# First modulation in one-tile groups, with repacked weights and zero products on TensorE

## The chip, the cores and the metric

The kernel runs on one core of one Trainium2 chip. The core has TensorE (PE, matrix products), VectorE (DVE), ScalarE (ACT), GpSimd (POOL) and SyncE (SP, which here only issues DMAs). The metric is the device time of one execution in microseconds (us). "Before" is given as the median of three runs.

## What is computed

The reference is a two-layer backbone over 256 latent tokens and 256 context tokens, with 1024 features. Layer 0 mixes tokens with a bidirectional mLSTM, layer 1 with latent attention; each is followed by a gated ConvFFN. Every sub-layer's input is first modulated by a shift and a scale that come from a condition vector. The change concerns the first of these modulations and the first matrix product behind it:

```python
ml = silu(c)     @ ada_w[0] + ada_b[0]    # 6 rows of 1024: shift, scale, gate, ...
mc = silu(c_ctx) @ ada_w[0] + ada_b[0]
hl = x   * (1 + ml[1]) + ml[0]
hc = ctx * (1 + mc[1]) + mc[0]
x_m = h @ w_up                             # h: hc and hl, 512 tokens; w_up: 1024 x 2048
```

## The kernel before

All activations are kept transposed: features on the 128 partitions, the 512 tokens along the free axis, so the 1024 features are eight *feature tiles*. Each fp32 product is made of three fp32r products (`mm3`, lines 312 to 314): both operands are split into a high part, which ACT makes by a cast (line 317), and a low part, which DVE makes by a subtraction (line 318); then high x high, high x low, low x high are accumulated.

The opening stage is `start_up`. It makes the modulation's shift and scale for all eight feature tiles, modulates the tokens, and meanwhile computes the first five (`NUP`) of the sixteen output tiles of `w_up`, called up 0 to up 4 here. The tiles of features are taken in four groups of two (`GROUPS`). For a group g the steps are:

- `S`: split the group's modulation weights. They are 1 MB a feature tile (1024 inputs x 128 features x shift and scale), so two SBUF tiles of 128x1024 a feature tile, four a group; each takes one ACT cast and one DVE subtraction (`ada_split`).
- `A`: products of the condition (as a stationary operand of 4 columns) with these parts, and a copy of the 4-row result out of PSUM by ACT (`ada_rows`, lines 402 and 405). The products have 512 columns for a group of two tiles; there are 16 of them.
- `T`: tiny transposes on TensorE that turn the rows into columns (`ada_T`, line 412).
- `M`: two small DVE additions (lines 422, 423), then for each feature tile the modulation itself (DVE for the context half, line 500; ACT for the latent half, line 502) and its split into `hT` (`mod_tiles`, `h_split`).
- `W` m: split of the weights of up m.
- two digits gm: the products of up m with the feature tiles of group g, three a feature tile.

In `start_up`, the strings `LOADS` and `STEPS` are orders written out by hand. `LOADS` is the order in which SP issues the loads: `a` g the modulation weights of group g, `x` g the transposed tokens of its tiles (256 KB each), `r` m the weights of up m (512 KB). `STEPS` is the order of work, and inside `manual_schedule` the queues of PE, DVE and ACT each hold their instructions in just this order; an instruction that waits holds up all that stand behind it on its engine. The modulation weights are read from `ada_w` as eight transfers of 256 KB a group, in pieces of 1 KB. `setup` loads the small parameters (`sm`) through SP's queue.

When the products of the five up tiles are done, `w_up` goes on with the other eleven, and from there on TensorE works nearly without a gap.

Of the kernel before, what the change touches and what calls it, by code (L numbers as in the profile page):

```python
# [7 lines left out]
F32 = mybir.dt.float32  # L8
F32R = mybir.dt.float32r
# [5 lines left out]
D = 1024  # L15
# [10 lines left out]
H1 = 8  # L26
# [5 lines left out]
NB, NRAW, NU = 3, 3, 31  # L32
# [9 lines left out]

NUP = 5
GROUPS = ((0, 2), (2, 4), (4, 6), (6, 8))
LOADS = [(c[0], int(c[1])) for c in "a0 r0 r1 x0 r2 a1 r3 r4 x1 a2 x2 x3 a3".split()]
STEPS = [(c[0], int(c[1])) for c in (
    "S0 W0 A0 T0 M0 W1 W2 S1 00 01 W3 W4 A1 03 T1 M1 02 04 10 11 S2 A2 12 T2 M2 13 14 21 "
    "S3 20 A3 24 T3 22 23 M3 31 32 33 34 30").split()]  # L50

TAIL = {"mout": 4, "fout0": 6, "aout": 7, "fout1": 6}
WIDE = {"mout": 5, "fout0": 6, "aout": 7, "fout1": 10}
# [67 lines left out]
def _pack(i):  # L121
    ids, _ = _plan()
    ws = np.zeros((len(ids), 128, CW), np.float32)
# [14 lines left out]
    for key, (n, cols) in ids.items():  # L138
        kind, a, c = key
        if kind == "up":  # L140
            b = _stat(i["m_w_up"][0], a, 0, 8)
        elif kind == "og":
            b = _mov(i["m_w_og"][0][:, a * 512:(a + 1) * 512], 2 * c, 2)
        elif kind == "gates":
            b = _stat(gz, 0, 8 * c, 8)
        elif kind == "v":
            b = _mov(i["m_w_v"][0][:, a * 512:(a + 1) * 512], 2 * c, 2)
        elif kind == "qk":
            b = _stat(i["m_w_qk"][0], a, 8 * c, 8)
        elif kind == "mout":  # L150
            b = _mov(i["m_w_out"][0], c, 1)
        elif kind in ("fin0", "fin1"):
            b = _stat(i["ffn_w_in"][int(kind[-1])], a + NF * c, 0, 8)
        elif kind in ("fout0", "fout1"):
            b = _mov(i["ffn_w_out"][int(kind[-1])], c, 1)
        elif kind == "dkv":
            b = _mov(i["a_w_dkv"][0], dkv_s[c], cols // 320)
        elif kind == "dq":
            b = _mov(i["a_w_dq"][0], 2 * c, 2)
        elif kind == "ukn":  # L160
            b = kn_blocks[:, c * 1024:(c + 1) * 1024]
        elif kind == "uv":
            b = _mov(uv, c, 1)
        elif kind == "uqn":
            b = qn_blocks[:, c * 1024:(c + 1) * 1024]
        elif kind == "uqr":
            b = _mov(uqr, 2 * c, cols // 512)
        elif kind == "aout":
            b = _mov(i["a_w_out"][0], c, 1)
        ws[n, :, :cols] = b  # L170

    def col(a):
        a = np.asarray(a)
        k = a.shape[-1] // 128
        a = a.reshape(a.shape[:-1] + (k, 128))
        return np.moveaxis(a, -1, 0).reshape(128, -1)
# [16 lines left out]
    for k, v in parts.items():  # L193
        off[k] = (o, v.shape[1])
        o += v.shape[1]
    sm = np.concatenate(list(parts.values()), axis=1).astype(np.float32)
# [10 lines left out]
    rope = np.stack([np.tile(cc, (1, H1)), np.tile(ss, (1, H1))], 0).astype(np.float32)  # L207
# [1 line left out]
    tok = np.concatenate([i["ctx"][0], i["x"][0]], 0)  # L209
    tokT = np.ascontiguousarray(tok.T.reshape(8, 128, T))  # L210
    arrays = {
        "ws": ws, "sm": np.ascontiguousarray(sm), "rope": np.ascontiguousarray(rope),
        "tok": np.ascontiguousarray(tok), "tokT": tokT,
        "ada_w": np.ascontiguousarray(i["ada_w"]), "ada_b": np.ascontiguousarray(i["ada_b"]),
        "ln_g": np.ascontiguousarray(i["ln_g"]).reshape(4, D),
# [68 lines left out]
class K:  # L284
# [66 lines left out]
    def setup(self):  # L351
        nc, p = self.nc, self.pool
        a = self.a
        self.sm = p.tile([128, a["sm"].shape[1]], F32, name="sm")
        nc.sync.dma_start(self.sm, a["sm"])
        b1 = self.smc("ada_b")[:, 8:16]
        nc.vector.tensor_scalar(b1, b1, 1.0, None, op0=ALU.add)
        jp = p.tile([128, 128], I32, tag="s2", name="jp", bufs=13)
        nc.gpsimd.iota(jp, pattern=[[1, 128]], base=0, channel_multiplier=-1)
        self.ident = p.tile([128, 128], F32, name="ident")  # L360
        nc.vector.tensor_scalar(self.ident, jp, 0.0, None, op0=ALU.is_equal)
        self.mask = p.tile([128, 2, 128], F32, name="mask")
        nc.vector.tensor_scalar(self.mask[:, 0], jp, 0.0, NEG, op0=ALU.is_gt, op1=ALU.mult)
        nc.vector.tensor_scalar(self.mask[:, 1], jp, 0.0, NEG, op0=ALU.is_lt, op1=ALU.mult)
        self.k1 = p.tile([128, 1], F32, name="k1")
        nc.vector.memset(self.k1, 1.0)
        self.keps = p.tile([128, 1], F32, name="keps")
        nc.vector.memset(self.keps, EPS)
        self.cond = p.tile([128, 8, 2], F32, name="cond")
        nc.scalar.activation(self.cond.rearrange("p a b -> p (a b)"), self.smc("cond"), AF.Silu)  # L370
        self.condr = p.tile([128, 8, 4], F32R, name="condr")
        self.split(self.condr[:, :, 0:2], self.condr[:, :, 2:4], self.cond)
        self.mod0 = p.tile([128, 2, 8, 2], F32, name="mod0")
        self.modc = {(0, c): self.mod0[:, c] for c in range(2)}
        self.gd = {}
        for l in range(2):
            for c in (3, 4) if l == 0 else (0, 1, 3, 4):
                self.modc[l, c] = p.tile([128, 8, 2], F32, name="mod%d%d" % (l, c))
            for c in range(6):
                self.gd[l, c] = self.dr.tile([2, D], F32, name="gd%d%d" % (l, c))  # L380

    def ada_split(self, g):
        r = []
        for w in self.adaw.pop(g):
            hi, lo = [self.pool.tile([128, 1024], F32R, tag="u", name="adas", bufs=NU) for _ in range(2)]
            self.split(hi, lo, w)
            r.append((hi, lo))
        return r

    def ada_rows(self, g, parts):  # L390

# [122 lines left out]
    def start_up(self):  # L514

        nc, st = self.nc, self.st
        self.hT = []
        self.xcd = self.dr.tile([16, 128, 512], F32, name="xcd")
        self.xm, self.xc = [], []
        w, ps, raws = [], [], []  # L520
        src = self.a["ada_w"][0]
        self.adaw, self.xT = {}, []
        for op, g in LOADS:
            f0, f1 = GROUPS[g] if op != "r" else (0, 0)
            if op == "a":
                wd = 128 * (f1 - f0)
                nk = 512 // wd
                self.adaw[g] = []
                for k in range(8):
                    if k % nk == 0:  # L530
                        t = self.uf("adaw")
                        self.adaw[g].append(t)
                    ap = bass.AP(tensor=src.tensor, offset=src.offset + k * 128 * 6 * D + f0 * 128,
                                 ap=[[6 * D, 128], [D, 2], [1, wd]])
                    c = k % nk * 2 * wd
                    nc.sync.dma_start(t[:, c:c + 2 * wd].rearrange("p (a b) -> p a b", a=2), ap)
            elif op == "x":
                for i in range(f0, f1):
                    x = self.s2("xT")
                    nc.sync.dma_start(x, self.a["tokT"][i])  # L540
                    self.xT.append(x)
            else:
                n, _ = st.ids["up", g, 0]
                r = self.pool.tile([128, 1024], F32, tag="raw" if g < 3 else "ar", name="raw0",
                                   bufs=NRAW if g < 3 else 2)
                nc.sync.dma_start(r, st.ws[n])
                raws.append(r)

        def wsplit(m):
            if m < 3:  # L550
                t = self.pool.tile([128, 2, CW], F32R, tag="w", name="w", bufs=NB)
                h, l = t[:, 0], t[:, 1]
            elif m == 3:
                h, l = [self.pool.tile([128, CW], F32R, tag="acc", name="w0", bufs=2) for _ in range(2)]
            else:
                h, l = [self.pool.tile([128, CW], F32R, tag="u", name="w0", bufs=NU) for _ in range(2)]
            self.split(h, l, raws[m])
            w.append((h, l))
            ps.append(self.ps("up"))

        def part(g, ms):
            for m in ms:
                for k in range(*GROUPS[g]):
                    c = slice(k * 128, (k + 1) * 128)
                    self.mm3(ps[m], (w[m][0][:, c], w[m][1][:, c]), (self.hT[k][:, 0], self.hT[k][:, 1]),
                             k == 0, k == 7)

        e = mybir.EngineType
        rows = {}
        with self.tc.manual_schedule(engines={e.PE, e.DVE, e.Activation}):  # L570
            for op, g in STEPS:
                if op == "S":
                    rows[g] = self.ada_split(g)
                elif op == "A":
                    rows[g] = self.ada_rows(g, rows[g])
                elif op == "T":
                    rows[g] = self.ada_T(g, rows[g])
                elif op == "M":
                    self.ada_cols(g, rows.pop(g))
                    self.mod_tiles(range(*GROUPS[g]))  # L580
                elif op == "W":
                    wsplit(g)
                else:
                    part(int(op), [g])
        for m in range(NUP):
            self.up_evac(m, ps[m])
# [22 lines left out]
    def w_up(self):  # L609
        st = self.st  # L610
        for m in range(NUP, 16):
            w = st.use(("up", m, 0))
# [755 lines left out]
def build(tc, off, a, out):  # L1368
    es = ExitStack()
    with es:  # L1370
# [4 lines left out]
        k.setup()  # L1375
        st.skip(NUP)
        k.start_up()
# [162 lines left out]
```

## Time and profile before

| what | value |
|---|---|
| median of 3 runs | 1444.35 us (1442.58 to 1446.5) |
| the profiled execution's own time | 1444.17 us |
| its span in the trace | 1442.4 us |
| TensorE busy | 1407.6 us, 98% |
| VectorE busy | 982.0 us, 68% |
| ScalarE busy | 643.1 us, 45% |
| bytes moved | 262.71 MB, mean 182 GB/s |

The time of an execution is the span and the 1.8 us around it. In rows of a timeline the first number is the start in us from the span's start, the second the length in us; "x4" means four instructions merged into one row; in brackets stands how long the engine sat idle before, and what released it. Matmul rows overlap: their length includes the way through the array, so the pace of a stream is the distance between starts. In a table by stretches of time each engine's busy time is followed by its number of instructions, then the granted TensorE clock (1.00 is full), the share of the DMA engines and what they moved.

### The profile page before, as it was taken

Reading aid. Unit: us, or ns where it says so; the run is one execution under the profiler, and the core shown is the slowest. Engines: PE = TensorE matmul, PEld = TensorE weight load, DVE = VectorE, ACT = ScalarE, POOL = GpSimd, SP = SyncE. Lnnn points to the kernel's source line nnn. Section 1 sums busy time; section 2 is a strip of 40 time slices with the busy share of each in tenths; the row PEclk is TensorE's granted clock in tenths of the full one; section 3 lists DMA queues with packets and bytes.
Section 4 is the critical chain, followed back from the end, with each engine's and each line's share of the span. In section 5 each row is a group of like instructions: output and inputs, shape, how many; then the busy total and the mean of one; then the engine's idle time right before and its main releaser. Section 6 shows DMA issues by size and latency. Waiting matters only on the chain.

```text
span 1442.4 us, 18843 instructions
## 1 busy us (share of the span) xinstructions
PE 1407.6 (98%) x7094; PEld 1177.4 (82%) x7094; DVE 982.0 (68%) x1451; ACT 643.1 (45%) x970; POOL 100.6 (7%) x185
## 2 busy tenths in 40 slices
PE   6999999999999999999999999999999989999997
PEld 3788888888888888877888888888888967899986
DVE  6796879976676676656787444444657787777755
ACT  6554232224334354465543333334455545455542
POOL 0011010003001010111001000000000011000000
PEclk9999999999999999999999999999999999999999
DMA  9476776777765545546635233435555334356763
GB/s 334 169 239 191 240 248 210 259 229 282 250 218 160 190 148 174 161 157 210 214 125 182 92 117 113 129 122 177 188 183 151 121 126 146 110 184 217 225 194 100
DMA packets 82828, 262.71 MB, mean 182 GB/s; under 512 B 11352, under 2 KB 19752, under 8 KB 82736
## 3 DMA queue, kind: packets, MB, share of 16 engines
q1 hardware_dynamic: 68304, 214.82, 46.3%
q0 software_dynamic: 14144, 46.17, 9.6%
q8 instruction: 55, 0.90, 0.3%
q10 hardware_dynamic: 288, 0.52, 0.1%
q14 instruction: 37, 0.30, 0.1%
HBM read 243.56 MB, written 17.91 MB: 181 GB/s over the span
## 4 chain that ended last, share of the span: by engine, by line
PE 68%; issue 18%; DMA 6%; DVE 4%; ACT 2%; POOL 2%; DVEq 0%; SPq 0%; POOLq 0%; ACTq 0%
PE fin L312 8%; PE fin L314 8%; PE fin L313 8%; PE y L313 6%; PE y L314 6%; PE y L312 5%; PE qk L314 4%; PE qk L312 4%; PE qk L313 4%; DMA raw<-in_ws 3%; DMA ar<-in_ada_w 2%; PE up L312 1%; PE up L314 1%; PE up L313 1%; DMA xcr<-xcd 1%
## 5 line engine op out<-in xcount | busy, mean ns | idle before, releaser
L257 DVE TENSOR_TENSOR w<-raw,w 128x1024 fp32r<-128x1024 f32 (+2 forms) x267 | 324.2, 1214 | 244.9 <-ACT w L256 244.0
L256 ACT CAST w<-raw 128x1024 fp32r<-128x1024 f32 (+2 forms) x267 | 278.9, 1045 | 437.2 <-PE tok L314 154.3
L314 PE MATMUL fin<-h,w 128*128 128x256 f32 (+1 forms) x696 | 231.6, 333 | 0.5 <-DVE w L257 0.5
L313 PE MATMUL fin<-h,w 128*128 128x256 f32 (+1 forms) x696 | 231.7, 333 | 0.0
L312 PE MATMUL fin<-h,w 128*128 128x256 f32 (+1 forms) x696 | 231.5, 334 | 0.0
L437 DVE SCALAR_TENSOR_TENSOR acc<-ar,cond,acc 128x1024 f32<-128x1024 f32 x112 | 140.5, 1279 | 35.5 <-DMA ar<-in_ada_w 35.1
L314 PEld LDWEIGHTS fin<-h,w 128*128 128x128 f32 x696 | 132.2, 190 | 13.8 <-DVE w L257 0.9
L313 PEld LDWEIGHTS fin<-h,w 128*128 128x128 f32 x696 | 132.2, 190 | 12.8 <-DVE h L992 0.2
L312 PEld LDWEIGHTS fin<-h,w 128*128 128x128 f32 x696 | 131.9, 190 | 13.1
L312 PE MATMUL qk<-xc,w 128*128 128x512 f32 x256 | 101.1, 395 | 0.0
L312 PE MATMUL tok<-w,xm 128*128 128x512 f32 x256 | 100.4, 392 | 0.0
L314 PE MATMUL qk<-xc,w 128*128 128x512 f32 x256 | 100.1, 391 | 0.3 <-DVE w L257 0.3
L313 PE MATMUL qk<-xc,w 128*128 128x512 f32 x256 | 99.9, 390 | 0.0
L314 PE MATMUL tok<-w,xm 128*128 128x512 f32 x256 | 99.7, 389 | 0.0
L313 PE MATMUL tok<-w,xm 128*128 128x512 f32 x256 | 99.6, 389 | 0.0
L312 PE MATMUL y<-w,act 128*128 128x512 f32 (+1 forms) x212 | 80.4, 379 | 0.0
L313 PE MATMUL y<-w,act 128*128 128x512 f32 (+1 forms) x212 | 80.1, 378 | 0.0
L314 PE MATMUL y<-w,act 128*128 128x512 f32 (+1 forms) x212 | 80.1, 378 | 0.0
L257 DVE TENSOR_TENSOR wu<-raw,wu 128x1024 fp32r<-128x1024 f32 x36 | 43.9, 1222 | 20.0 <-ACT wu L256 19.5
L314 PEld LDWEIGHTS qk<-xc,w 128*128 128x128 f32 x256 | 48.1, 188 | 10.6 <-DVE w L257 0.7
L312 PEld LDWEIGHTS tok<-w,xm 128*128 128x128 f32 x256 | 48.0, 188 | 10.3
L314 PEld LDWEIGHTS tok<-w,xm 128*128 128x128 f32 x256 | 48.0, 188 | 10.1
(354 smaller groups left out, 2771.1 us busy)
## 6 DMA issues: line engine op xcount, KB each, us to landing
raw<-in_ws SPq DMA_DIRECT2D x300, 512.0 KB, 3.9
ar<-in_ada_w SPq DMA_DIRECT2D x80, 512.0 KB, 4.6
adaw<-in_ada_w SPq DMA_DIRECT2D x32, 256.0 KB, 6.4
xcd<-cv POOLq DMA_DIRECT2D x16, 256.0 KB, 3.9
od<-o POOLq DMA_DIRECT2D x16, 256.0 KB, 4.0
vd<-v POOLq DMA_DIRECT2D x16, 256.0 KB, 3.7
xcr<-xcd POOLq DMA_DIRECT2D x16, 256.0 KB, 6.2
vr<-vd POOLq DMA_DIRECT2D x16, 256.0 KB, 4.6
```

The costliest lines, as they stand in the source:

```text
L256: k.nc.scalar.copy(h[:, :cols], raw[:, :cols])
L257: k.nc.vector.tensor_sub(l[:, :cols], raw[:, :cols], h[:, :cols])
L312: mm(out, w[0], x[0], start=start, stop=False)
L313: mm(out, w[0], x[1], start=False, stop=False)
L314: mm(out, w[1], x[0], start=False, stop=stop)
L437: nc.vector.scalar_tensor_tensor(acc[j], w, s, acc[j], op0=ALU.mult, op1=ALU.add)
```

## The change

The groups become six: four of one feature tile, then two of two tiles. `LOADS` and `STEPS` are rewritten for them. A group of one tile has 16 products of 256 columns in `A`, a copy of 4x256, and two transposes.

The modulation weights that the opening needs are packed on the host into a new array `ad` of 16 blocks of 128x1024 in the order in which they are used, and each block is loaded by one contiguous transfer of 512 KB. The bytes are the same. `sm` moves from SP's queue to ACT's.

Two kinds of steps are new. `D` n puts n products of a zero tile (128x128 stationary, 512 columns) into a PSUM bank that nobody reads. `H` g makes the high part of the first weight block of group g ahead of the rest of its split; `ada_split` then skips what is done. The zero tile is cleared by DVE at the start of `setup`.

```diff
-GROUPS = ((0, 2), (2, 4), (4, 6), (6, 8))
-LOADS = [(c[0], int(c[1])) for c in "a0 r0 r1 x0 r2 a1 r3 r4 x1 a2 x2 x3 a3".split()]
-STEPS = [(c[0], int(c[1])) for c in (
-    "S0 W0 A0 T0 M0 W1 W2 S1 00 01 W3 W4 A1 03 T1 M1 02 04 10 11 S2 A2 12 T2 M2 13 14 21 "
-    "S3 20 A3 24 T3 22 23 M3 31 32 33 34 30").split()]
+GROUPS = ((0, 1), (1, 2), (2, 3), (3, 4), (4, 6), (6, 8))
+LOADS = [(c[0], int(c[1])) for c in "a0 x0 r0 a1 x1 r1 a2 x2 r2 a3 x3 r3 r4 a4 x4 a5 x5".split()]
+STEPS = [(c[0], int(c[1:])) for c in (
+    "D12 S0 W0 A0 D2 T0 D10 H1 M0 S1 00 D3 A1 D2 T1 W1 D1 01 H2 M1 D3 S2 10 11 W2 A2 02 T2 12 H3 M2 20 21 22 S3 "
+    "W3 A3 03 T3 13 23 M3 W4 S4 30 31 32 33 04 14 24 34 A4 T4 M4 S5 40 41 42 A5 43 T5 44 M5 50 51 52 53 54").split()]
...
+    aw = i["ada_w"][0][:, :2 * D].reshape(8, 128, 2, D)
+    ad = []
+    for f0, f1 in GROUPS:
+        g = aw[:, :, :, f0 * 128:f1 * 128].transpose(1, 0, 2, 3).reshape(128, -1, 1024)
+        ad.extend(g[:, j] for j in range(g.shape[1]))
+    ad = np.ascontiguousarray(np.stack(ad))
...
-        nc.sync.dma_start(self.sm, a["sm"])
+        nc.scalar.dma_start(self.sm, a["sm"])
+        self.zero = p.tile([128, 512], F32R, tag="s2", name="zero", bufs=13)
+        nc.vector.memset(self.zero.bitcast(F32), 0.0)
...
+    def ada_hi(self, g, n):
+
+        r = self.adas.setdefault(g, [])
+        for w in self.adaw[g][len(r):n]:
+            hi, lo = [self.pool.tile([128, 1024], F32R, tag="u", name="adas", bufs=NU) for _ in range(2)]
+            self.nc.scalar.copy(hi, w)
+            r.append((hi, lo))
+
     def ada_split(self, g):
-        r = []
-        for w in self.adaw.pop(g):
-            hi, lo = [self.pool.tile([128, 1024], F32R, tag="u", name="adas", bufs=NU) for _ in range(2)]
-            self.split(hi, lo, w)
-            r.append((hi, lo))
-        return r
+        ws = self.adaw[g]
+        for i, w in enumerate(ws):
+            self.ada_hi(g, i + 1)
+            hi, lo = self.adas[g][i]
+            self.nc.vector.tensor_sub(lo, w, hi)
+        del self.adaw[g]
+        return self.adas.pop(g)
...
-                wd = 128 * (f1 - f0)
-                nk = 512 // wd
                 self.adaw[g] = []
-                for k in range(8):
-                    if k % nk == 0:
-                        t = self.uf("adaw")
-                        self.adaw[g].append(t)
-                    ap = bass.AP(tensor=src.tensor, offset=src.offset + k * 128 * 6 * D + f0 * 128,
-                                 ap=[[6 * D, 128], [D, 2], [1, wd]])
-                    c = k % nk * 2 * wd
-                    nc.sync.dma_start(t[:, c:c + 2 * wd].rearrange("p (a b) -> p a b", a=2), ap)
+                for j in range(2 * f0, 2 * f1):
+                    t = self.uf("adaw")
+                    nc.sync.dma_start(t, self.a["ad"][j])
+                    self.adaw[g].append(t)
...
+        idle = self.ps("idle")
...
             for op, g in STEPS:
-                if op == "S":
+                if op == "D":
+                    for _ in range(g):
+                        nc.tensor.matmul(idle, self.zero[:, 0:128], self.zero, start=True, stop=True)
+                elif op == "H":
+                    self.ada_hi(g, 1)
+                elif op == "S":
                     rows[g] = self.ada_split(g)
```

More of the change, by code (lines that the diff above doesn't have):

```diff
@@ L211, in _pack @@
     arrays = {
-        "ws": ws, "sm": np.ascontiguousarray(sm), "rope": np.ascontiguousarray(rope),
+        "ws": ws, "ad": ad, "sm": np.ascontiguousarray(sm), "rope": np.ascontiguousarray(rope),
         "tok": np.ascontiguousarray(tok), "tokT": tokT,
@@ L520, in start_up @@
         w, ps, raws = [], [], []
-        src = self.a["ada_w"][0]
-        self.adaw, self.xT = {}, []
+        self.adaw, self.adas, self.xT = {}, {}, []
         for op, g in LOADS:
```

## The prediction

> **What bounds the kernel now.** I read the page first.
>
> ```profile
> span 1442.4 us, 18843 instructions
> ...
> PE 1407.6 (98%) x7094; PEld 1177.4 (82%) x7094; DVE 982.0 (68%) x1451; ACT 643.1 (45%) x970; POOL 100.6 (7%) x185
> ```
>
> TensorE is the bound; only 34.8 us of the span lie outside its busy rows. The table by stretches says where the opening's share is.
>
> ```profile
> 0.00:10.00 10.00, 1.60 (x4) 0.42 (x5) 2.79 (x9) 4.09 (x6) 0.43 (x5) 1.00 0.80 237
> 10.00:20.00 10.00, 6.83 (x22) 2.39 (x21) 6.83 (x11) 6.93 (x10) 0.00 (x0) 0.97 1.06 376
> 20.00:30.00 10.00, 9.86 (x37) 5.05 (x37) 9.44 (x11) 7.12 (x9) 0.00 (x0) 0.86 1.07 369
> ```
>
> The gaps (8.4 and 3.2 us) lie before 20 us; the third row has hardly any. Next its timeline, in three places: the start, the two speeds, the end of the stage.
>
> ```profile
> 7.72 0.59 PE L402 MATMUL adar<-adas,condr 128*4 128x512 f32 x1 [7.72 <-ACT adas L317]
> ...
> 14.98 0.41 PE L412 MATMUL adat<-ident,adarow 4*128 4x4 f32 x4 [0.67 <-ACT adarow L405]
> 17.12 0.50 PE L312 MATMUL up<-hT,w 128*128 128x512 f32 x1 [1.74 <-ACT hT L317]
> ...
> 21.05 0.63 PE L313 MATMUL up<-hT,w 128*128 128x512 f32 x1
> 21.48 0.63 PE L314 MATMUL up<-hT,w 128*128 128x512 f32 x1
> ...
> 31.54 0.39 PE L312 MATMUL up<-hT,w 128*128 128x512 f32 x1
> 31.76 0.39 PE L313 MATMUL up<-hT,w 128*128 128x512 f32 x1
> ...
> 34.95 3.86 PE L402 MATMUL adar<-adas,condr 128*4 128x512 f32 x16
> ...
> 51.58 0.50 PE L312 MATMUL up<-hT,w 128*128 128x512 f32 x1
> ...
> 61.10 0.39 PE L314 MATMUL up<-hT,w 128*128 128x512 f32 x1
> 61.33 0.39 PE L312 MATMUL up<-hT,w 128*128 128x512 f32 x1
> ```
>
> A 512-column product takes 0.43 us at half clock (21.05 to 21.48) and 0.228 at full clock: 41 steps from 51.58 to 61.10 average 0.232 with the slow first one, 31.54 to 31.76 shows 0.22. Behind T3 stand 12 + 30 = 42 products, so the opening's last one starts at 61.10 and `w_up` takes over at **61.3 us**. From there TensorE is busy without a break, so what the change does to the time is how far it moves this 61.3.
>
> **The change, part by part.** TensorE's useful work stays: 120 up products, and as many columns of modulation products (64x256 + 32x512 = 64x512), and 16 transposes. What changes is when they may run. The chain of one group needs these lengths, ACT's first, then DVE's:
>
> ```profile
> 3.28 0.21 ACT L370 ACTIVATE cond<-sm 128x16 f32<-128x16 f32 x1 [1.25 <-DMA sm<-in_sm]
> ...
> 6.63 1.04 ACT L317 CAST adas<-adaw 128x1024 fp32r<-128x1024 f32 x1 [2.90 <-DMA adaw<-in_ada_w]
> ...
> 16.45 0.62 ACT L317 CAST hT<-xT 128x512 fp32r<-128x512 f32 x1
> ...
> 38.85 0.58 ACT L405 COPY adarow<-adar 4x512 f32<-4x512 f32 x1 [3.06 <-PE adar L402]
> 40.97 1.09 ACT L502 ACTIVATE xT<-xT,mod 128x256 f32<-128x256 f32 x2 [1.54 <-DVE mod L423]
> 41.97 1.12 ACT L317 CAST hT<-xT 128x512 fp32r<-128x512 f32 x2
> 43.00 3.90 ACT L317 CAST adas<-adaw 128x1024 fp32r<-128x1024 f32 x4
> ```
>
> ```profile
> 17.10 0.69 DVE L318 TENSOR_TENSOR hT<-xT,hT 128x512 fp32r<-128x512 f32 x1 [0.87 <-ACT hT L317]
> ...
> 31.51 1.29 DVE L318 TENSOR_TENSOR hT<-xT,hT 128x512 fp32r<-128x512 f32 x2 [0.90 <-ACT hT L317]
> ...
> 40.56 0.17 DVE L422 TENSOR_TENSOR adt<-adat,sm 128x8 f32<-128x8 f32 x1 [2.94 <-PE adat L412]
> 40.77 0.17 DVE L423 TENSOR_TENSOR mod<-adat,adt 128x8 f32<-128x8 f32 x1
> 40.97 0.74 DVE L500 TENSOR_SCALAR xT<-xT,mod 128x256 f32<-128x256 f32 x2
> 42.60 1.29 DVE L318 TENSOR_TENSOR hT<-xT,hT 128x512 fp32r<-128x512 f32 x2 [0.90 <-ACT hT L317]
> 44.08 4.63 DVE L318 TENSOR_TENSOR adas<-adaw,adas 128x1024 fp32r<-128x1024 f32 x4 [0.18 <-ACT adas L317]
> ```
>
> A block's cast is 1.04 (0.95 apart in a row of four), its subtraction 1.23 (1.13 apart). Three numbers are not in this trace as such:
>
> ```profile
> 0.75 0.39 SPq L355 DMA_DIRECT2D sm<-in_sm  x1
> ...
> 1260.04 0.28 PE L313 MATMUL fin<-h,w 128*128 128x256 f32 x1
> 1260.16 0.28 PE L314 MATMUL fin<-h,w 128*128 128x256 f32 x1
> ...
> raw<-in_ws SPq DMA_DIRECT2D x300, 512.0 KB, 3.9
> ...
> 10.00:12.00 2.00, 2.00 (x6) 0.46 (x4) 1.73 (x2) 1.66 (x2) 0.00 (x0) 1.00 1.02 405
> ...
> 36.00:38.00 2.00, 2.00 (x11) 0.71 (x9) 1.62 (x2) 0.00 (x0) 0.00 (x0) 1.00 1.09 348
> ```
>
> - A modulation product of 256 columns: 0.12, from the FFN's pace (1260.04 to 1260.16); at most the 0.23 of 512 columns (34.95: 16 in 3.7), which would put 1.8 us on each one-tile group. I take 0.12.
> - The copy of 4x256: at least half of 0.58, at most all; I take 0.37, as 256 elements fewer save 0.21 by the casts (1.04 for 1024, 0.62 for 512).
> - The landing of the first block: at the earliest like a weight block in steady state, issue at 0.75, where `sm` stands now, + 3.9 = 4.7 (page's row); at the latest as now, just before the cast at 6.63. I take 5.5, and 0.39 MB/us from there, near the 405 GB/s at 10 us, where 4 KB pieces move, not the 348 at 36 us, where 1 KB pieces do. All 13.1 MB are then in by 38 us, and after the first group no step waits for them.
>
> Moving `sm` takes 0.4 us off SP's queue ahead of the first block, which is in the landing above, and puts as much on ACT's, where nothing is due before `sm` itself lands (3.28). The 32 transfers of the modulation weights become 16; SP only issues, and the transfers, not the issues, fill the time. Clearing the zero tile is one DVE instruction ahead of 3.28, where DVE is idle. If that cover were gone each would cost under half a microsecond, once. The 33 zero products take 12 x 0.43 at the start, before any block is split, and otherwise at most 10 x 0.23 = 2.3 us behind T0, where the chain from T0 to the first up product took 17.12 - 14.98 = 2.1 us anyway: at most 0.2 us on the path.
>
> Now the order of `STEPS`, laid over these lengths (0.04 us for a hand-over).
>
> *Group 0.* Blocks at 5.5 and 6.8, casts to 6.6 and 7.9, subtractions to 9.2, A0 to 9.5. ACT has W0's cast ahead of the copy (r0 lands at 8.9, cast to 10.0), copy to 10.6, T0 10.9; DVE has W0's subtraction ahead, to 11.2. Additions to 11.5, modulation to 12.2, cast to 12.8, subtraction to 13.5: the first up product runs at **13.1**, not 17.1. This is what the change wins.
>
> *Groups 1 to 3.* On DVE the subtractions of the next group stand behind `M`, so each group pays the whole chain in series: 2.36 for two subtractions, 0.4 last products, 0.4 copy, 0.5 transposes, 0.4 additions, 0.6 modulation, 0.65 cast, 0.7 subtraction, together 6.0 us, plus what stands in between: W1 (its cast at 17.2 and its subtraction to 19.5) ahead of M1's additions, 2.2 us; the products 02 ahead of T2, 0.7; A3's 16 products and 03, which start only at 30.3, 1.3. The first product on a new tile then comes at 21.1, 27.7 and **35.0**. The cover for these waits is products on one, two, three tiles, which are few; TensorE mostly waits or multiplies zeros. Before, two tiles were paid by one chain: tiles 2 and 3 were ready at 31.5.
>
> *From 35.0*, step by step on TensorE: 24 up products 5.5, half a microsecond for the low part of tile 3: 41.0. A4, 16 x 0.228: 44.6. Here the order is "A4 T4 M4 S5 40", with nothing in between: copy 0.58 and hand-overs, T4 at 45.4, done 45.8; additions 0.4, two modulations 1.0, cast 0.6, with hand-overs 2.3: 48.0. Before, products stood at each of these places. 18 up products and 0.5 for a low part: 52.6. A5: 56.3. 43, T5, 44: 59.4. M5's chain from T5 ends at 60.3, so 0.9 of waiting. 30 up products and 0.5: **67.6**.
>
> The same stepping applied to the old order gives 60.6 where the trace has 61.3, so it is short by 0.7 rather than long. On top comes the clock.
>
> ```profile
> 12.57:15.99 3.42, 2.14 (x11) 1.00 1.04 388
> 15.99:19.40 3.41, 1.73 (x4) 1.00 1.10 351
> 19.40:22.82 3.42, 3.21 (x8) 0.50 1.07 381
> ```
>
> Stretches of 3.41 us are granted full or half clock; the one behind a stretch with 4 products ran at half, the one behind a stretch with 11 did not. From 44.6 to 48.0 the new order has four transposes and nothing else, so I expect one stretch at half clock around 48 to 51, where 8 products run in place of 15: 1.5 us. End **69.1**, 7.8 us later than 61.3. On the profiled execution's 1444.17 us this is **1452.0 us**; its distance to the median shown, 1444.35, is 0.2 and I leave it.
>
> The Trainium skill (TensorE: Matmul & The Clock Gate, Part 1) says that the clock falls back after at least one idle window of about 3.4 us. Read strictly, a wait of 3.4 us with transposes in it would not trip it, and the end would be 67.6, 1450.5 us. The trace does not agree with the strict reading: the stretch to 19.40 was half busy and was still followed by half clock.
>
> **Rivals.**
>
> *Not slower: the early chains are shorter than in series.* If the subtractions of group g+1 ran on DVE ahead of M of group g, 2.4 us would leave each chain, and three chains would bring tile 3 at 28 instead of 35. The 32.6 us behind it then end at 60.6: 1443.4 us; and as the splits of M4 and M5 would come early too, up to 4 us of the waits there go as well: 1439.5 us. It decides from 28.7 downwards (28.7 + 32.6 = 61.3). For it: blocks land long before, and `H` does run one cast early. Against it: rows at 40.97 to 44.08 have the subtractions behind M's, exactly as written, and `H` moves casts only.
>
> *Hardly slower.* Products find no half clock, the first block lands at 4.7 and waits at M4 are shorter by a microsecond: 67.6 - 0.8 - 1.0 = 65.8, or +4.5: 1448.7; with a little more, inside the bound below.
>
> *The zeros don't keep the clock.* If products with zeros do not count as work, the early stretches hold few others and most run at half clock: at 0.215 for 0.12, the 16 products of A1, A2 and A3 take 1.5 us longer each, less about one where a stretch is granted full: 69.1 + 3.5 = 72.6, or 1455.5 us. The trace has no such products, so nothing speaks for it but that.
>
> **How the numbers follow.** Forecast 0.64; zeros without effect 0.12; hardly slower 0.14; not slower 0.10. 0.3%, or 4.3 us, is what a measurement of this kernel can tell from no change. Of the hardly slower I count 0.08 within it, of the not slower 0.03 within and 0.07 as faster: faster 0.07, same 0.11, slower 0.64 + 0.12 + 0.06 = 0.82. The forecast's own range is 1449 (no half clock, early landing) to 1454 (0.7 short, late landing); to hold 8 in 10 it goes from 1447.5 to 1456.
>
> **What would show it.** First up product near 13; first products on the 2nd, 3rd and 4th tile near 21, 28 and 35; a wait of TensorE of 2 to 3 us behind T4, released by ACT's cast of `hT`; `w_up` starting near 69. It is wrong if tile 3's first product comes before 30, or if TensorE has no gap between 40 and 60.

## The result, and the profile after

The changed kernel takes 1452.56 us (median of 8 runs, 1450.88 to 1460.01) against 1444.88 us for the kernel before on the same chips (8 runs). The medians differ by 7.7 us, where 7.8 were forecast. The ratio worked out from the runs is 1.0061, with a 95% interval of 1.0046 to 1.0076, so slower by 6.6 to 11.0 us: the agreement to 0.1 us is closer than this measurement can tell.

The page of the changed kernel, its span and TensorE's share:

```profile
span 1449.7 us, 18953 instructions
...
PE 1416.5 (98%) x7159; PEld 1186.8 (82%) x7159; DVE 982.2 (68%) x1456; ACT 643.3 (44%) x972; POOL 100.5 (7%) x185
```

The span is 7.3 us longer, and TensorE's busy time 8.9 us longer: the 33 zero products account for about that, 4.5 us at the start and 21 x 0.23 = 4.8 behind it. Its timeline in the opening (start, length, idle before and releaser; `mm3` has moved to lines 321 to 323):

```profile
1.46 4.47 PE L588 MATMUL idle<-zero 128*128 128x512 f32 x12 [1.46 <-DVE keps L379]
...
13.02 0.39 PE L321 MATMUL up<-hT,w 128*128 128x512 f32 x1
...
20.70 0.50 PE L321 MATMUL up<-hT,w 128*128 128x512 f32 x1 [0.36 <-ACT hT L326]
...
27.31 0.50 PE L321 MATMUL up<-hT,w 128*128 128x512 f32 x1 [0.83 <-ACT hT L326]
...
34.68 0.50 PE L321 MATMUL up<-hT,w 128*128 128x512 f32 x1
...
40.79 3.86 PE L422 MATMUL adar<-adas,condr 128*4 128x512 f32 x16
45.32 0.41 PE L432 MATMUL adat<-ident,adarow 4*128 4x4 f32 x4 [0.67 <-ACT adarow L425]
47.82 0.50 PE L321 MATMUL up<-hT,w 128*128 128x512 f32 x1 [2.09 <-ACT hT L326]
...
49.63 0.63 PE L322 MATMUL up<-hT,w 128*128 128x512 f32 x1
50.06 0.63 PE L323 MATMUL up<-hT,w 128*128 128x512 f32 x1
...
61.82 0.50 PE L321 MATMUL up<-hT,w 128*128 128x512 f32 x1 [0.51 <-ACT hT L326]
...
69.05 0.39 PE L323 MATMUL up<-hT,w 128*128 128x512 f32 x1
69.28 0.39 PE L321 MATMUL up<-hT,w 128*128 128x512 f32 x1
```

The rows at 13.02, 20.70, 27.31 and 34.68 are the first products on the four one-tile groups, 47.82 and 61.82 those on the two-tile groups. The 120th product starts at 69.05, so `w_up` begins at 69.28, where it began at 61.33 before: 7.95 us later, and in these two executions the rest of the program is 0.65 shorter. The first product does come 4.1 us earlier (13.02 for 17.12). That lead is lost by the fourth tile, whose products begin at 34.68; the kernel before begins on the third and fourth tile together at 32.22:

```profile
32.22 0.39 PE L312 MATMUL up<-hT,w 128*128 128x512 f32 x1
```

In the changed kernel's trace up to 70 us the only waits for a transfer are those for `sm` and one of 0.8 us, of `W0`'s cast at 8.29. So the new order of the loads is not what holds it.

Two rows of the changed kernel's ACT, M4's modulation and cast, and two of its DVE show what stands in a chain: ACT's are the wait behind T4; `W1`'s subtraction at 17.87 holds M1's addition to 19.01, while T1's transposes had ended at 17.2.

```profile
46.17 1.09 ACT L522 ACTIVATE xT<-xT,mod 128x256 f32<-128x256 f32 x2 [0.90 <-DVE mod L443]
47.17 1.12 ACT L326 CAST hT<-xT 128x512 fp32r<-128x512 f32 x2
...
17.87 1.23 DVE L327 TENSOR_TENSOR w<-raw,w 128x1024 fp32r<-128x1024 f32 x1 [2.42 <-ACT w L326]
19.01 0.15 DVE L442 TENSOR_TENSOR adt<-adat,sm 128x4 f32<-128x4 f32 x1
```

The clock, by stretches of the changed kernel (the stretch, its length, TensorE's busy time and instructions, granted clock, DMA share, GB/s): the stretch with the wait behind T4 holds 1.09 us of work, and the next one is granted half of the full clock.

```profile
45.57:48.98 3.41, 1.09 (x6) 1.00 0.00 0
48.98:52.40 3.42, 3.42 (x10) 0.50 0.00 0
```

### The profile page after: what moved, and what is told of

It reads as the page before. It is cut to its first block, busy times and chain, and to the rows that moved or that the text cites. A ratio compares the mean times of both kernels' runs of the same rounds, so it can differ in the third digit from the quotient of the medians.

```text
span 1449.7 us, 18953 instructions
## 1 busy us (share of the span) xinstructions
PE 1416.5 (98%) x7159; PEld 1186.8 (82%) x7159; DVE 982.2 (68%) x1456; ACT 643.3 (44%) x972; POOL 100.5 (7%) x185
## 4 chain that ended last, share of the span: by engine, by line
PE 65%; issue 18%; DMA 6%; DVE 6%; ACT 3%; POOL 2%; DVEq 0%; POOLq 0%; ACTq 0%
PE fin L321 8%; PE fin L323 8%; PE fin L322 8%; PE y L322 5%; PE y L323 5%; PE y L321 5%; PE qk L323 4%; PE qk L321 4%; PE qk L322 4%; DMA raw<-in_ws 3%; DMA ar<-in_ada_w 2%; PE adar L422 1%; PE up L322 1%; DMA xcr<-xcd 1%; DVE w L266 1%
## 5 line engine op out<-in xcount | busy, mean ns | idle before, releaser
L323 PEld LDWEIGHTS fin<-h,w 128*128 128x128 f32 x696 | 132.2, 190 | 13.8 <-DVE w L266 0.9
L323 PEld LDWEIGHTS qk<-xc,w 128*128 128x128 f32 x256 | 48.1, 188 | 11.4 <-DVE w L266 1.4
L323 PEld LDWEIGHTS tok<-w,xm 128*128 128x128 f32 x256 | 48.1, 188 | 10.1
L321 PEld LDWEIGHTS qk<-xc,w 128*128 128x128 f32 x256 | 48.1, 188 | 10.0
```

The costliest lines, as they stand in the source:

```text
L321: mm(out, w[0], x[0], start=start, stop=False)
L323: mm(out, w[1], x[0], start=False, stop=stop)
```

## Experiments

The edits change only the opening, so the start of `w_up` (the 121st up product) in each profile is the sharpest measure; e8 alone waits again soon behind it. "Two-tile order" is the groups, loads and steps of before.

| run | what it is | first up product | w_up starts |
|---|---|---|---|
| before | | 17.12 | 61.33 |
| after | | 13.02 | 69.28 |
| e1_packed_old | packed blocks, `sm` on ACT, two-tile order | 16.06 | 60.27 |
| e2_packed_old_zeros | the same with zeros | 15.11 | 59.18 |
| e3_no_zeros | after without zeros | 13.74 | 73.06 |
| e4_late_filled | after with the wait at M4 covered | 13.04 | 64.95 |
| e5_subs_first | after with S ahead of M | 15.34 | 83.06 |
| e6_sm_on_sp | after with `sm` first on SP | 15.70 | 71.92 |
| e7_before_zeros | before with zeros | 17.00 | 61.09 |
| e8_best | two-tile, zeros, new order, `sm` on SP | 16.19 | 60.84 |
| e9_w1_early | after with W1 behind S1 | 13.34 | 67.96 |
| e10_best2 | as e8, `sm` on ACT, other last order | 15.02 | 59.30 |
| e11_sm_behind | after, `sm` on SP behind the first blocks | 15.34 | 72.72 |
| e12_before_sm_act | before with `sm` on ACT | 16.05 | 60.23 |

Six of these were executed once, and their times decide nothing: e5 1468.93 us, e6 1461.89 and e7 1446.25, beside a median of 1444.02 for the kernel before; e9 1448.37, e11 1460.30 and e12 1448.78, beside 1446.32. e12 is not faster here although its `w_up` starts 1.1 us earlier; the last section shows why a single time can't tell.

**The parts that are not the order.** The first two runs take the two-tile order back, with `LOADS` and `STEPS` of before; e2 adds three `D` steps to it.

```diff
-GROUPS = ((0, 1), (1, 2), (2, 3), (3, 4), (4, 6), (6, 8))
+GROUPS = ((0, 2), (2, 4), (4, 6), (6, 8))
...
-    "S0 W0 A0 T0 M0 W1 W2 S1 00 01 W3 W4 A1 03 T1 M1 02 04 10 11 S2 A2 12 T2 M2 13 14 21 "
+    "D12 S0 W0 A0 D2 T0 D8 M0 W1 W2 S1 00 01 W3 W4 A1 03 T1 M1 02 04 10 11 S2 A2 12 T2 M2 13 14 21 "
```

> The changed kernel's packed loads and `sm` on ACT's queue, with the two-tile groups, load order and step order of before, no zeros. Theory (one-tile groups in series and uncovered waits cost the time): the packing is harmless and a little good; first up product near 15 instead of 17.1, w_up starts at 58.5 to 60, time 1.5 to 3 us under before. Rival (the repacked loads or the moved `sm` cost the time): w_up starts at 66 or later, time 5 us or more above before.

> As the first, with 12 zero products ahead, 2 behind A0 and 8 behind T0. Theory: the zeros cost nothing and hold the clock, so no half-clock stretch before 60; w_up starts at 58 to 59, up to 1.5 us ahead of the first run, time 2 to 3 us under before. Rival (zeros cost the time): w_up at least 2 us later than in the first run.

e1 measured 1442.32 us, ratio to before 0.999 (0.9974 to 1.0006), which is no clear difference; e2 1441.89 us, ratio 0.9977 (0.996 to 0.9994). Both start `w_up` 0.2 to 0.3 us later than expected. So neither the packing, nor the move of `sm`, nor the zeros cost the time: with all three and the old order the kernel is 0.2% faster than before, and `w_up` starts 10.1 us earlier than in the changed kernel. The loss is in the groups and their order. e2's first product, at 15.11, also shows that 2.0 of the 4.1 us by which the changed kernel's came earlier are not due to the one-tile groups.

What the zeros do in the old order is seen in `A0`. Its last 15 products, first in e1, then in e2:

```profile
7.80 5.44 PE L419 MATMUL adar<-adas,condr 128*4 128x512 f32 x15 [0.67 <-DVE adas L403]
```

```profile
7.88 4.26 PE L421 MATMUL adar<-adas,condr 128*4 128x512 f32 x15 [0.87 <-DVE adas L405]
```

They end 1.1 us earlier in e2, and that is the whole gain at `w_up` (60.27 to 59.18).

**The zeros.** e3 leaves out every `D` step, e7 puts zeros into the kernel before.

> The changed kernel without any zero product. Theory: they cover clock, not work; without them the early chains run in part at half clock, first product on the fourth tile 1 to 3 us later than 34.7, w_up starts at 70 to 72.5 (69.3 with them). Rival (the zeros hold up useful products): w_up starts at 67 or earlier and the time falls by 2 us or more.

e3 by stretches (TensorE alone, columns as above):

```profile
14.29:17.70 3.41, 3.24 (x13) 0.50 1.03 405
...
21.12:24.53 3.41, 2.58 (x5) 0.50 1.02 407
24.53:27.95 3.42, 3.42 (x15) 0.50 1.02 404
```

Three early stretches at half clock where the changed kernel has none; `w_up` starts 3.8 us later, at 73.06 a little past the expected 70 to 72.5; time 1459.62 us, ratio to before 1.0095 (1.0064 to 1.0125). Products with zeros count as work for the clock here: in the changed kernel 12 of them, alone on TensorE, take 4.47 us (the row at 1.46) where half clock throughout would take 12 x 0.43 = 5.1.

> The kernel before with zero products alone (12 ahead, 2 behind A0, 8 behind T0), loads as before. Theory: no half-clock stretch at 19 to 23 and A0 at full clock; w_up at 59.5 to 60.5 against 61.3. Rival (in the old order the waits, not the clock, set it): 61.3 or later.

61.09: a miss, though the half-clock stretch did go. In e7 `A0` has the full clock too, but its products wait for subtractions of blocks that land one by one, here the second and the fourth:

```profile
10.16 1.08 PE L404 MATMUL adar<-adas,condr 128*4 128x512 f32 x4 [0.78 <-DVE adas L318]
...
13.19 0.86 PE L404 MATMUL adar<-adas,condr 128*4 128x512 f32 x3 [0.47 <-DVE adas L318]
```

So the first up product comes only 0.1 us earlier (17.00 for 17.12). The waits of TensorE's weight loads between 17 and 28 us, first in e7, then in the kernel before (engine, line, waited for: us in total, times, longest):

```profile
PEld adar L404 <- DVE adas L318: 3.1, 4, 1.4
```

```profile
PEld adar L402 <- DVE adas L318: 2.2, 4, 0.6
```

TensorE gets through the first up products faster and then waits longer for the subtractions of group 1. In that place DVE was the limit, so the clock cost next to nothing: from the first up product to `w_up` it is 44.1 us in e7 and e2, and 44.2 in the kernel before and e1, whose early products run at half clock. What zeros are worth in the old order is won in `A0`, and only when its blocks are there.

**The waits at M4.**

```diff
-... M3 W4 S4 30 31 32 33 04 14 24 34 A4 T4 M4 S5 40 ...
+... M3 S4 W4 30 31 32 33 A4 04 T4 14 24 34 M4 S5 40 ...
```

> The changed kernel with S4 ahead of W4, A4 ahead of products 04 and T4 ahead of products 14, 24, 34. Theory: the 3 us of waits at T4 and M4 are covered and the half-clock stretch behind them falls away; w_up starts at 64.5 to 65.5, 4 to 5 us earlier than in the changed kernel, and still 3 to 4 us later than before. Rival (the wait only moves to M5 or to the splits of group 5): w_up within 1.5 us of 69.3.

TensorE's timeline of e4 around the place and at the end:

```profile
42.56 0.41 PE L431 MATMUL adat<-ident,adarow 4*128 4x4 f32 x4
...
45.79 0.50 PE L321 MATMUL up<-hT,w 128*128 128x512 f32 x1 [0.23 <-DVE hT L326]
...
64.95 0.39 PE L320 MATMUL up<-hT,w 128*128 128x512 f32 x1
```

T4 has no wait ahead of it, no stretch from there to `w_up` is at half clock, and `w_up` starts 4.3 us earlier: 2.8 us of waits (0.67 + 2.09), and the remaining 1.5 is put down to the clock (3.41 us at half clock can cost up to 1.7). The time is 1450.57 us, ratio to before 1.0037 (1.0018 to 1.0056): still slower.

**What stands in the chains.**

```diff
-... H1 M0 S1 00 D3 A1 D2 T1 W1 D1 01 H2 M1 ...
+... H1 M0 S1 W1 00 D3 A1 D2 T1 D1 01 H2 M1 ...
```

> The changed kernel with W1 moved from behind T1 to behind S1, so that its cast and subtraction no longer stand between T1 and M1. Theory (the chains are serial, what stands in one delays all behind it): first product on the second tile at 19.0 instead of 20.7, on the fourth at 33.0 instead of 34.7, w_up 1.7 us earlier, at 67 to 68. Rival (the later waits absorb it): w_up at 69 or later.

e9's first product on the fourth tile, and its start of `w_up`:

```profile
33.32 0.51 PE L320 MATMUL up<-hT,w 128*128 128x512 f32 x1
...
67.96 0.39 PE L320 MATMUL up<-hT,w 128*128 128x512 f32 x1
```

One split of 2.2 us moved out of the second tile's chain brings the later stages 1.3 to 1.4 us forward (34.68 to 33.32, 69.28 to 67.96); nothing further back absorbs it. Expected were 1.7 on the fourth tile. The first product itself is 0.3 us late in this execution (13.34), as the 12 zeros at the start take 5.49 us here for 4.47, at half clock for longer.

```diff
-... T0 D10 H1 M0 S1 00 ... 01 H2 M1 D3 S2 10 11 ... 12 H3 M2 20 21 22 S3 ...
+... T0 D10 S1 M0 00 ... 01 S2 M1 D3 10 11 ... 12 S3 M2 20 21 22 ...
```

> The changed kernel with the whole split of the next group ahead of M (S1, S2, S3 in place of H1, H2, H3). The prediction's rival says that this takes 2.4 us out of each chain: fourth tile's first product near 28, w_up near 61. Laid over the measured lengths the theory says the opposite: casts and subtractions of a block that lands later stand ahead of the modulation on ACT and DVE, so the first product on the first tile comes at 15.3 instead of 13.0, on the fourth at 42, w_up at 75 to 80.

e5's first products on the first, third and fourth tile:

```profile
15.34 0.64 PE L320 MATMUL up<-hT,w 128*128 128x512 f32 x1 [2.12 <-ACT hT L325]
...
38.64 0.50 PE L320 MATMUL up<-hT,w 128*128 128x512 f32 x1 [3.55 <-ACT hT L325]
...
47.56 0.50 PE L320 MATMUL up<-hT,w 128*128 128x512 f32 x1
```

The fourth tile was expected at 42 and comes at 47.56. `w_up` starts at 83.06, 13.8 us later than in the changed kernel, past the expected 75 to 80: more waiting also brought six stretches of 3.41 us at half clock, where the changed kernel has one. So the way out that the prediction gave its first rival is, in this order, the wrong way.

**The queue of `sm`.** In the changed kernel the first casts went at once, one behind the other, but only when the condition was ready:

```profile
5.14 0.22 ACT L381 ACTIVATE cond<-sm 128x16 f32<-128x16 f32 x1 [2.66 <-DMA sm<-in_sm]
...
5.50 1.99 ACT L398 CAST adas<-adaw 128x1024 fp32r<-128x1024 f32 x2
```

```diff
-        nc.scalar.dma_start(self.sm, a["sm"])
+        nc.sync.dma_start(self.sm, a["sm"])
```

> The changed kernel with `sm` back at the head of SP's queue. In the changed kernel `sm` landed at 5.1 and the first cast stood behind it. Theory: `sm` lands near 3.3, the first block near 5.2, and the first cast starts 0 to 0.4 us earlier; w_up 0 to 0.4 us earlier than 69.3. Rival (the move to ACT's queue is a good part of the loss): first cast a microsecond or more earlier.

> The kernel before with `sm` on ACT's queue and nothing else changed. If the queue of `sm` is worth 1 us or more by itself, the first up product comes at 16 or earlier and w_up at 60.5 or earlier. If it takes the packed blocks as well, both stay within 0.5 us of 17.1 and 61.3.

> The changed kernel with `sm` on SP's queue, but issued behind the first group's two blocks. If what matters is that the blocks go first, the second block is split as early as in the changed kernel (second subtraction done by 9) and w_up stays within 0.7 us of 69.3. If what matters is that two queues issue at the start, the second block is as late as with `sm` at the head of SP's queue (split at 7.9, w_up at 71 or later).

The first casts of e6, each now behind its own block:

```profile
5.19 1.05 ACT L398 CAST adas<-adaw 128x1024 fp32r<-128x1024 f32 x1 [1.51 <-DMA adaw<-in_ad]
7.89 1.05 ACT L398 CAST adas<-adaw 128x1024 fp32r<-128x1024 f32 x1 [1.65 <-DMA adaw<-in_ad]
```

The first cast does start 0.3 us earlier, as expected, but `w_up` misses both sides: the second block's cast is 1.4 us later (6.45 in the changed kernel), and with a half-clock stretch from 10.4 the loss grows to 2.6 us. The transfers from 4 to 5 us (length, clock, DMA share, GB/s), in order: the kernel before, e6, e12, e11, the changed kernel.

```profile
4.00:5.00 1.00, 1.00 0.74 186
```

```profile
4.00:5.00 1.00, 1.00 0.92 274
```

```profile
4.00:5.00 1.00, 1.00 1.09 383
```

```profile
4.00:5.00 1.00, 1.00 1.00 409
```

```profile
4.00:5.00 1.00, 1.00 1.07 425
```

With `sm` at the head of SP's queue the transfers behind it falter; with `sm` on ACT's queue, or on SP's behind the blocks, they don't. In the kernel before, the move alone is worth 61.33 - 60.23 = 1.1 us. e11 fits neither of its two cases: the two blocks were there in time (their casts at 6.55 run in a row), but `sm` came later, at 6.2, and held them. So in these runs the order decides about the falter, and the second queue lets `sm` and the blocks both be first. Why the transfers falter stays open, and the falter alone does not make the second block of e6 1.4 us late: from 1 to 6 us e6 moves 1242 KB and the changed kernel 1350, which is 0.3 us at 400 GB/s.

**Two tiles with another step order.** e8 and e10 are the two-tile order with packed blocks, zeros and another step order. The steps of e8:

```diff
+    "D12 S0 W0 A0 D2 T0 D7 M0 00 S1 W1 W2 W3 A1 01 T1 M1 S2 02 03 11 S3 13 A2 10 W4 A3 T2 12 04 T3 M2 M3 "
+    "22 23 14 21 20 24 34 32 33 31 30"
```

e10 has `D8` in place of `D7`, ends with "22 23 21 20 14 31 32 30 33 24 34", and leaves `sm` on ACT's queue.

> Two-tile groups, packed loads, `sm` on SP's queue, zeros ahead and behind T0, and a step order in which no wait of TensorE is left behind the second group. Theory: w_up at 58 to 59, 2.5 to 3.3 us ahead of before, time 0.15 to 0.25% under before. Rival (what is won in the opening is lost in the stage behind it, whose splits wait for the weights of the last products): TensorE waits between 58 and 75 and the time is that of before.

> Two-tile groups, packed loads, `sm` on ACT's queue, zeros, the reordered steps of the eighth run, with the products of up 0 to 2 ahead of those of up 3 and 4 in the last group so that their weight buffers come free early. Theory: w_up at 58 to 59.2, no wait behind it up to 80, time 2.5 to 3.3 us under before, like the second run or half a microsecond better. Rival: TensorE waits again for a split behind 60.

e8 has `sm` on SP's queue, which puts its first product at 16.19, and behind the opening it waits as its rival said. Up 0 to 2 hold the buffers that the next weights take, and this order ends with "34 32 33 31 30": ACT's cast for these weights waits 8.6 us for the last product of up 2, until 56.91, and the casts behind it come late:

```profile
56.91 1.05 ACT L264 CAST w<-raw 128x1024 fp32r<-128x1024 f32 x1 [8.62 <-PE up L322]
...
69.05 0.50 PE L320 MATMUL up<-hT,w 128*128 128x512 f32 x1 [1.70 <-ACT w L264]
```

Its ratio is 1.0007 (0.9992 to 1.0021), with 1445.35 us. e10 has neither: `w_up` at 59.30, a little past the expected 59.2, no wait from there to 80, 1442.04 us, ratio 0.9978 (0.9964 to 0.9993). e2 does as well with the old order. Both are 0.2% under the kernel before, so the new step order adds nothing that can be seen.

## Why the prediction was right

*Groups 0 to 3.* Forecast 13.1, 21.1, 27.7, 35.0; measured 13.02, 20.70, 27.31, 34.68. Each one-tile group pays the whole chain in series, and what stands in one delays all behind it (e9: 1.3 us for W1; e5: more ahead of `M` is worse). That 13.02 meets 13.1 is in part luck. T0 came at 10.40, not 10.9. Then the zeros held the first product: the high part of the first tile was done at 12.45 (11.83 + 0.62), the last of ten zero products let go at 13.02, 0.5 us later, where the prediction allowed 0.2.

```profile
11.83 0.62 ACT L326 CAST hT<-xT 128x512 fp32r<-128x512 f32 x1
```

```profile
10.62 2.57 PE L588 MATMUL idle<-zero 128*128 128x512 f32 x10
```

*From 35.0.* T4 forecast 45.4, measured 45.32; the first product behind M4 48.0 and 47.82; `w_up` 69.1 and 69.28. The wait at M4, 2.3 us forecast, shows as 2.09 and was taken away in e4.

*The clock.* One stretch at half clock was forecast at 48 to 51; it lay at 48.98 to 52.40. That it was just one is not sure in every execution: in e11, which has the same steps, two such stretches follow each other there, from 49.77 to 56.60. The Trainium skill (TensorE: Matmul & The Clock Gate, Part 1) speaks of at least one idle window of about 3.4 us; here a window with 1.09 us of work in it was enough, so the measurement decides against the strict reading.

*What the pieces sum to.* Measured one by one: `sm` on ACT's queue -1.1 (e12), packing 0.0 (e1 against e12: 60.27 and 60.23), zeros -1.1 (e2 against e1), then the one-tile order +10.1 (69.28 against e2's 59.18). The shares hold for this order of adding them: zeros alone on the kernel before gave 0.2 (e7). Packing shows nothing without zeros, as `A0`'s last 15 products run in large part at half clock and take 5.4 to 5.5 us in both e1 and e12 (4.26 in e2); packing with zeros against zeros alone, at the same queue of `sm`, was not run in the old step order. Of the 10.1, e4 takes back 4.3 and e9 1.3; if the two add up, 4.5 are left, which are put down to the chains in series. That remainder was not taken away by an experiment of its own.

*What was mis-sized.* The move of `sm` was put at 0.4 us for the first block's landing and at nothing on ACT, with `sm` still landing before 3.28. On ACT's queue it lands at 5.1, and yet the move is a gain: 1.1 us in the old order, 2.6 in the new (e6, in part by the clock). The schedule came out right all the same, by luck: the first cast, put at 5.5 as a landing between two bounds, did start at 5.50, but `sm` set it and not the block; the second cast came at 6.45, not 6.8. And 0.39 MB/us for packed blocks was about right (405 GB/s in e3's rows).

*The rivals.* Zeros do keep the clock (e3; without any zeros `w_up` starts at 73.06, near the 72.6 of the rival in which they have no effect). The "not slower" rival had its mechanism the wrong way round (e5). Of what the "hardly slower" rival needs, nothing moved the time: there was a half-clock stretch, the first cast started at 5.50, and the wait at M4 was 2.09. The step from the opening to the whole time held: 7.95 us there, 7.7 us in the median.

## What to carry to other kernels

Finer groups bring the first result earlier and each pay the full latency of the chain, so they help only while other work fills every chain: write the order out against measured lengths, look for places where a chain of three engines stands with nothing on the bound engine, and count what is queued ahead of each link. Here such waits of 2.8 us cost another 1.5 or so through the clock. Zero products are a cheap cover for the clock, not for work, and pay only where TensorE, and not a transfer or another engine, is late next (e2 and e3 against e7).

## What the hardware showed beyond that

The scatter of this kernel's runs is in part the clock too. Around 1170 us, in the attention's chain, TensorE idles; what is granted behind it differs between executions of kernels that there do the same. First e2, then e1 (busy times of all five engines):

```profile
1166.49:1169.91 3.42, 0.82 (x6) 0.34 (x2) 3.22 (x5) 0.78 (x2) 0.00 (x0) 1.00 0.21 22
1169.91:1183.56 13.65, 11.53 (x36) 8.41 (x37) 8.34 (x25) 5.42 (x14) 0.00 (x0) 0.50 0.20 73
```

```profile
1168.90:1172.31 3.41, 0.00 (x0) 0.00 (x0) 3.32 (x10) 1.78 (x5) 0.00 (x0) 1.00 0.56 173
1172.31:1175.72 3.41, 2.91 (x11) 2.40 (x11) 2.95 (x9) 2.23 (x6) 0.00 (x0) 0.50 0.37 139
1175.72:1185.96 10.24, 10.24 (x54) 7.16 (x54) 8.24 (x17) 4.81 (x10) 0.55 (x1) 1.00 0.24 72
```

Half clock for 13.65 us in one and 3.41 us in the other. The 10.24 us more at half clock are 5.1 us less work. So e2's profiled span is 1444.1 us and e1's 1440.1, although e2's opening is 1.1 us shorter (1440.1 - 1.1 + 5.1 = 1444.1); their medians stand as the openings do, 1441.89 and 1442.32. A single time of such a run says little about a change of a few us, and the place in the profile that the change touches says much.
